# The two maps of differential attention combined by one VectorE instruction, and the output projection and norms of a hybrid encoder layer laid out anew

## The chip, the cores and the metric

The kernel runs on one core of a Trainium2 chip. The metric is the device time of one execution in microseconds (us). The kernel before took 3208.94 us (median of three runs, 3205.79 to 3213.26). The execution that was profiled took 3200.6 us; its span, from the first to the last instruction, is 3198.8 us.

## The reference

One encoder layer on two sequences that share their weights: a prompt of 512 tokens and a sample of 1024, each token 1024 wide, float32 throughout.

```python
h = rmsnorm(x, norm_pre_mix)
q, k, v, z, xbc, dt, gates = split(h @ w_in)
# attention: 8 heads, two maps each; scores get a bias by relative position
p = softmax(q @ k.T * scale + bias)          # per head and map
att = rmsnorm((p[0] - lam * p[1]) @ v, subln_w) * (1 - lam_init)
y = ssd(conv(xbc), dt) ... gated by z, normed # the state-space branch
m = (g0 * (att @ w_proj_attn) + g1 * (y @ w_proj_ssm)) @ w_out
x = x + rmsnorm(m, norm_post_mix)
h = rmsnorm(x, norm_pre_ffn)
f = (silu(h @ w_gate) * (h @ w_up)) @ w_down  # d_ff = 2816
x = x + rmsnorm(f, norm_post_ffn)
```

## The kernel before, in words

Every large product is done with three matrix multiplications on operands split into a high and a low part (`split`, lines 134 to 146: a ScalarE copy makes the high part, a VectorE or GpSimd subtraction the low part; `gemm`, lines 167 to 170, issues the three). The 1536 tokens are three chunks of 512: chunk 0 is the prompt, chunks 1 and 2 are the sample. Intermediate results go to DRAM tensors (`att_d`, `part_d`, `x2_d`, `h2_d`, `ff_d` and others). All loads and stores are issued by one queue, SyncE's (SP), in order.

The order of instructions on each engine is not the order of the text: the tile framework schedules with a model of times. Each instruction has a place in the text, and of those that are ready in the model the one with the earliest place goes first; a tile of a pool is given out when one of its buffers is free. Once planned, each engine runs its list in order.

Stages, by the time in the profiled span:

- **Up to about 1340 us**: first norm, projections, attention of the prompt woven into them, convolution and state-space scan.
- **Attention of the sample** (about 1345 to 1842 us). `heads` calls `attention` for 8 heads of 8 query tiles. For a query tile and each of the two maps: score matmuls into PSUM, a VectorE instruction that adds the bias and finds the maximum (L297), Exp on ScalarE (L300). Then the maps are combined: reciprocal and scale (L303, L304), and pm0 + scale * pm1, whose first half is one VectorE instruction (L307) and whose second half is two GpSimd instructions (L306, L309). Eight transposes follow, split again (L316, L317), and the product with v. `run` weaves a generator, `side_work`, between the steps of attention: after each of the 64 steps it advances it by `RATIO` = 0.5 steps. Side work has 32 steps of 24 matmuls: the attention projection of the prompt and the state-space projection of all three chunks (`gated`), stored in `part_d`.
- **Output projection and norms** (1842 to about 2175 us). `load_merged(0)` makes the operand of the prompt; `att_scale(1)` computes the scale of the sample's attention when its last head is done and stores it in `r_d`; `load_att(c)` loads a head of a chunk and its scales, multiplies (L357) and splits, head by head, through three buffers of the tag `araw`. `merge(c)` projects the scaled attention of a sample chunk (8 blocks of 24 matmuls) and adds `part_d`. `out_proj` multiplies by `w_out` (16 blocks of 24 matmuls) into four tiles that stay in SBUF, and `norms` does both norms on these tiles, transposes the result (L1083) and stores it in `h2_d`. The operands are pairs of 16 KB tiles out of a pool `big` of seven.
- **Gate and up products** (2101 to about 2806 us), by a seven-product scheme: `Operands` builds seven operands of 768 tokens from `h2_d` (two groups of tokens), `weights(jb)` builds seven weight operands of one of 22 blocks, `gate_up` does the seven products of 12 matmuls and combines them. Two blocks of the first group (`NPRE`) come ahead of `norms(2)` in the text and use Tanh for silu; the other blocks use buffers of a pool `fw` that is opened after the pool `mp` of the norms has closed.
- **Down product and last norm** (from 2806 us).

The text's order in the third stage is this, and the change rewrites it:

```python
m0 = load_merged(0); att_scale(1, ...); aT1 = att(1)
t0 = out_proj(m0);   m1 = merge(1, aT1); norms(0, t0)
aT2 = att(2); t1 = out_proj(m1); m2 = merge(2, aT2); norms(1, t1)
ops = Operands(0, wk, "araw", 3); ops.build_first(); ops.build(("b21",), ...)
t2 = out_proj(m2); ops.build(("t4",), ...); ops.build(("b22",), ...)
# two gate_up blocks, norms(2, t2); pool fw opens; the other blocks
```

Of the kernel before, what the change touches and what calls it, by code (L numbers as in the profile page):

```python
# [10 lines left out]
F32 = mybir.dt.float32  # L11
# [7 lines left out]
P = 128  # L19
D = 1024  # L20
# [12 lines left out]
VSH = 4  # L33
PU = (1, 1)
OT = ("gt", 2)
NG = 2
YE = ("act_pool",) * 4
RATIO = 0.5
# [4 lines left out]
NPRE = 2  # L43
CB = (1, 1)
RWB = 7
NW = 0
NKEEP = 1
# [31 lines left out]
def hybrid_trunk_kernel(ctx: ExitStack, tc: tile.TileContext, a: dict, y_prompt, y_sample):  # L79
# [35 lines left out]
    part_d = dram.tile([D, T], F32, name="part_d")  # L115
    x2_d = dram.tile([T, D], F32, name="x2_d")
# [150 lines left out]
    def attention(base, SL, h, got, pend, zq, msq, qk, pp, at, qr, s_ps, t_ps, o_ps):  # L267
# [7 lines left out]
        for qc in range(SL // 512):  # L275
            ops = o_ps.tile([P, 512], F32, tag="o", name="o")
            for q2 in range(2):
                aT = [at.tile([P, 2, 4, 256], F32R, tag=f"aT{b0}", name="aT", bufs=2 - b0 // 4)
                      for b0 in range(0, nkb, 4)]
                for u in range(2):  # L280
# [24 lines left out]
                    ca, cb = slice(0, SL * VSH // 8), slice(SL * VSH // 8, SL)  # L305
                    G.tensor_scalar(pm[1][:, cb], pm[1][:, cb], zs[:, 1:2], 0.0, op0=ALU.mult, op1=ALU.add)  # L306
                    V.scalar_tensor_tensor(pm[0][:, ca], pm[1][:, ca], zs[:, 1:2], pm[0][:, ca],  # L307
                                           op0=ALU.mult, op1=ALU.add)
                    last_add.append(G.tensor_add(pm[0][:, cb], pm[0][:, cb], pm[1][:, cb]))  # L309
# [494 lines left out]
    zq, msq = [ap.tile([P, 8, 8], F32, name=n) for n in ("zq", "msq")]  # L804
    with ExitStack() as ph2:
# [62 lines left out]

        side = side_work()
# [7 lines left out]
    with ExitStack() as ph3:  # L877
        big = ph3.enter_context(tc.tile_pool(name="big", bufs=7, reuse_waits="tile"))
        wk = ph3.enter_context(tc.tile_pool(name="wk", bufs=2, reuse_waits="tile"))
        wy = ph3.enter_context(tc.tile_pool(name="wy", bufs=1, reuse_waits="tile"))  # L880
        mm = ph3.enter_context(tc.tile_pool(name="mm", bufs=6, space=PSUM, reuse_waits="tile"))
# [5 lines left out]

        def big_pair():
            return [big.tile([P, KB, 512], F32R, tag="big", name="big") for _ in range(2)]

        def load_merged(c):
            hi, lo = big_pair()
            for k in range(0, KB, 2):
                both = mp.tile([P, 2, 512], F32, tag="mt", name="both", bufs=4)
                load(out=both, in_=part_d[k * P:(k + 2) * P, c * 512:(c + 1) * 512].rearrange("(a p) t -> p a t", p=P))
                S.activation(out=hi[:, k:k + 2], in_=both, func=AF.Copy, scale=0.5)
                V.scalar_tensor_tensor(lo[:, k:k + 2], both, 0.5, f(hi[:, k:k + 2]), op0=ALU.mult, op1=ALU.subtract)
            return hi, lo
# [141 lines left out]
        with ExitStack() as ph3a:  # L1040
# [69 lines left out]
            for jb in range(NPRE):  # L1110
                gate_up(0, jb, ops.all(), w[jb], mp, 1, False)
# [105 lines left out]
```

## Time and profile before

| what | value |
|---|---|
| median of three runs | 3208.94 us |
| the profiled execution | 3200.6 us |
| its span | 3198.8 us |
| mean granted TensorE clock | 0.979 |
| TensorE matmul busy | 3040.4 us, 95% |
| VectorE busy | 1814.7 us, 57% |
| ScalarE busy | 1256.6 us, 39% |
| GpSimd busy | 880.0 us, 28% |
| DMA | 430.39 MB, 43.1% of 16 engines' span on SP's queue |

How to read the rows: "L307 DVE ... x64 | 66.5, 1039 | 1.6" is a group of 64 instructions of line 307 on VectorE, 66.5 us busy, 1039 ns each on the mean, with 1.6 us of idle time ahead of them. PE is TensorE, PEld its weight loads, DVE VectorE, ACT ScalarE, POOL GpSimd, SPq SyncE's queue. Matmuls are pipelined and their ends are modelled, so a busy PE is not a PE at its peak.

### The profile page before, as it was taken

How to read it: one execution, taken by the hardware profiler on the slowest of the kernel's cores; microseconds unless marked ns; L12 is line 12 of the kernel's file. 1: busy time of each engine (PE TensorE's matmuls, PEld its weight loads, DVE VectorE, ACT ScalarE, POOL GpSimd, SP SyncE). 2: the span in 40 equal slices, each digit the busy share in tenths (PEclk: the TensorE clock that was granted, in tenths of full speed). 3: DMA queues.
4: the chain of work that ended last, by engine and by line, in shares of the span. 5: the costliest groups of instructions: out<-in, count | busy, mean ns of one | idle time of the engine just before them, and what ended most of it. 6: DMA issues, size and time to landing. Idle time of an engine off the chain costs nothing. (4 is left out here: it accounts for less than half of the span.)

```text
span 3198.8 us, 44610 instructions
## 1 busy us (share of the span) xinstructions
PE 3040.4 (95%) x16667; PEld 2671.8 (84%) x16667; DVE 1814.7 (57%) x2953; ACT 1256.6 (39%) x2301; POOL 880.0 (28%) x712
## 2 busy tenths in 40 slices
PE   7999999999999999899999998979999899989998
PEld 7988887888887778677788787868999899978787
DVE  5214443455328995387777855686667766632444
ACT  4103333333303433366666645543333333332343
POOL 0003332000233442277655500023333433210100
PEclk9999999999999999999999999988999999999999
DMA  4633333123554445755545147644333333363454
GB/s 148 195 99 113 111 101 109 57 78 106 155 166 143 145 141 154 209 156 169 163 140 187 34 141 238 228 130 136 103 98 109 92 103 98 109 201 97 123 163 132
DMA packets 443170, 430.39 MB, mean 135 GB/s; under 512 B 25233, under 2 KB 360306, under 8 KB 441842
## 3 DMA queue, kind: packets, MB, share of 16 engines
q1 hardware_dynamic: 442953, 427.55, 43.1%
q8 instruction: 131, 2.15, 0.3%
q14 instruction: 86, 0.70, 0.1%
HBM read 315.40 MB, written 120.44 MB: 136 GB/s over the span
## 5 line engine op out<-in xcount | busy, mean ns | idle before, releaser
L168 PE MATMUL acc<-hT,whi 128*128 128x512 f32 x1056 | 422.6, 400 | 3.3 <-ACT st L458 3.3
L169 PE MATMUL acc<-hT,whi 128*128 128x512 f32 x1056 | 417.6, 395 | 0.0
L170 PE MATMUL acc<-hT,wlo 128*128 128x512 f32 x672 | 263.8, 392 | 0.0
L300 ACT ACTIVATE pt<-pt,nm 128x1024 f32<-128x1024 f32 (+1 forms) x192 | 193.2, 1007 | 125.1 <-DVE nm L297 115.3
L168 PEld LDWEIGHTS acc<-hT,whi 128*128 128x128 f32 x1056 | 199.6, 189 | 48.8 <-issue 5.8
L297 DVE CUSTOM_DVE_ANT_0 pt<-s,tb 128x1024 f32<-128x1024 f32 (+1 forms) x192 | 196.9, 1041 | 68.3 <-PE s L295 50.1
L169 PEld LDWEIGHTS acc<-hT,whi 128*128 128x128 f32 x1056 | 199.6, 189 | 42.5 <-issue 3.6
L168 PE MATMUL acc<-whi,hT 128*128 128x256 f32 x768 | 224.9, 293 | 0.9 <-ACT hT L207 0.5
L170 PE MATMUL acc<-whi,hT 128*128 128x256 f32 x768 | 224.6, 293 | 0.4 <-DVE hT L208 0.3
L169 PE MATMUL acc<-wlo,hT 128*128 128x256 f32 x768 | 223.8, 292 | 0.0
L170 PE MATMUL d<-dhi,fl 128*128 128x512 f32 x528 | 207.8, 394 | 8.7 <-DVE fl L137 8.7
L168 PE MATMUL d<-dhi,fh 128*128 128x512 f32 x528 | 207.5, 393 | 7.8 <-ACT fh L136 7.8
L169 PE MATMUL d<-dlo,fh 128*128 128x512 f32 x528 | 207.2, 392 | 0.0
L137 DVE TENSOR_TENSOR fl<-raw,fh 128x896 fp32r<-128x896 f32 (+1 forms) x72 | 86.0, 1195 | 200.1 <-ACT fh L136 200.1
L136 ACT CAST whi<-wraw 128x1024 fp32r<-128x1024 f32 (+1 forms) x115 | 116.0, 1037 | 201.1 <-PE acc L169 84.1
L168 PE MATMUL mm<-op,wy 128*128 128x384 f32 x528 | 178.8, 339 | 9.4 <-ACT op L136 8.9
L170 PE MATMUL mm<-op,wy 128*128 128x384 f32 x528 | 178.7, 338 | 0.0
L169 PE MATMUL mm<-op,wy 128*128 128x384 f32 x528 | 178.3, 338 | 0.0
L306 POOL TENSOR_SCALAR pt<-pt,zs 128x512 f32<-128x512 f32 (+1 forms) x96 | 94.3, 982 | 281.8 <-DVE zs L304 240.3
L137 DVE TENSOR_TENSOR wlo<-wraw,whi 128x1024 fp32r<-128x1024 f32 x80 | 95.4, 1222 | 114.2 <-ACT whi L136 104.9
L136 ACT CAST fh<-raw 128x896 fp32r<-128x896 f32 (+1 forms) x72 | 70.7, 982 | 227.3 <-PE d L169 212.7
L170 PE MATMUL acc<-hT,whi 128*128 128x512 f32 x384 | 157.3, 410 | 0.0
(360 smaller groups left out, 8452.8 us busy)
## 6 DMA issues: line engine op xcount, KB each, us to landing
wraw<-in_w_in_dram SPq DMA_DIRECT2D x60, 512.0 KB
wraw<-in_w_gate_up_dram SPq DMA_DIRECT2D x92, 256.0 KB
raw<-ff_d SPq DMA_DIRECT2D x48, 448.0 KB
wr<-in_w_gate_up_dram SPq DMA_DIRECT2D x80, 256.0 KB
ff_d<-c SPq DMA_DIRECT2D x88, 192.0 KB
g_d<-st SPq DMA_DIRECT2D x48, 256.0 KB
xg<-xs_d SPq DMA_DIRECT2D x48, 256.0 KB
gt<-g_d SPq DMA_DIRECT2D x48, 256.0 KB
```

The source lines that it names most:

```text
L136: S.copy(hi, raw)
L137: V.tensor_sub(lo, raw, f(hi))
L168: TE.matmul(ps, ah, bh, start=(i == 0), stop=False)
L169: TE.matmul(ps, ah, bl, start=False, stop=False)
L170: TE.matmul(ps, al, bh, start=False, stop=(i == n - 1))
L297: V.tensor_tensor_reduce(out=pt[:], in0=sps[:], in1=tb[:, off:off + SL], scale=-1.0, scalar=3.0e38, op0=ALU.add, op1=ALU.min, accum_out=nm ...
L300: S.activation(out=pt, in_=pt, func=AF.Exp, bias=nm[:, m:m + 1], scale=-1.0, accum_out=(z0, zs[:, 0:1])[m])
L306: G.tensor_scalar(pm[1][:, cb], pm[1][:, cb], zs[:, 1:2], 0.0, op0=ALU.mult, op1=ALU.add)
```

## The change

- **Maps.** The combination of the two maps is one VectorE instruction on the whole width; GpSimd does none of it. `VSH` goes.
- **Side work.** The prompt's output projection becomes 16 more steps of the side work, through the one PSUM buffer `f`; `RATIO` is 0.75. Its operand `m0` takes the side work's tile `yT`.
- **Norms through memory.** `out_proj` stores its result in a new DRAM tensor `mo_d`; `norms` is a generator of 16 steps that loads 128x512 pieces of it (tag `nt`, four buffers, which `merge` uses for `pt` too), stores `x2_d` by halves, loads it again for the second norm, transposes and stores `h2_d`. The norms of the last chunk are advanced by one step after each gate-and-up block.
- **Operands.** The pool `big` has nine pieces of 12 KB. An operand of gate and up is one piece; a pair for a projection is three (`Part` finds the place). Each operand loads its own terms (40 loads a group rather than 20), all additions are VectorE's, and raw tiles come from `fw` (six buffers).
- **Pools.** `mp` is gone, `fw` is open for the whole stage; no block is done ahead with Tanh.

```diff
-RATIO = 0.5
+RATIO = 0.75
...
-                    ca, cb = slice(0, SL * VSH // 8), slice(SL * VSH // 8, SL)
-                    G.tensor_scalar(pm[1][:, cb], pm[1][:, cb], zs[:, 1:2], 0.0, op0=ALU.mult, op1=ALU.add)
-                    V.scalar_tensor_tensor(pm[0][:, ca], pm[1][:, ca], zs[:, 1:2], pm[0][:, ca],
-                                           op0=ALU.mult, op1=ALU.add)
-                    last_add.append(G.tensor_add(pm[0][:, cb], pm[0][:, cb], pm[1][:, cb]))
+                    last_add.append(V.scalar_tensor_tensor(pm[0], pm[1], zs[:, 1:2], pm[0], op0=ALU.mult, op1=ALU.add))
...
+    def out_proj(c, mT, pool, psum):
+        for p0 in range(0, D, 256):
+            w = split_panel(a["w_out"][0][:, p0:p0 + 256])
+            for j in range(4):
+                ps = psum()
+                gemm_tm(ps, w, mT, slice(j * P, (j + 1) * P))
+                mo = pool.tile([P, 512], F32, tag="gt", name="mo")
+                S.copy(mo[:, 0:256], ps)
+                S.activation(out=mo[:, 256:512], in_=ps, func=AF.Square, accum_out=sums[c][:, j, p0 // 256:p0 // 256 + 1])
+                r0 = c * 512 + j * P
+                store(out=mo_d[r0:r0 + P, p0:p0 + 256], in_=mo[:, 0:256])
+                yield
...
+            m0 = yt.tile([P, 2, KB, 512], F32R, tag="yT", name="m0", bufs=1)
+            for k in range(0, KB, 2):
+                both = rp.tile([P, 2, 512], F32, tag="wraw", name="both")
+                load(out=both, in_=part_d[k * P:(k + 2) * P, 0:512].rearrange("(a p) t -> p a t", p=P))
+                S.activation(out=m0[:, 0, k:k + 2], in_=both, func=AF.Copy, scale=0.5)
+                V.scalar_tensor_tensor(m0[:, 1, k:k + 2], both, 0.5, f(m0[:, 0, k:k + 2]), op0=ALU.mult, op1=ALU.subtract)
+            yield from out_proj(0, (m0[:, 0], m0[:, 1]), yt, lambda: f_ps.tile([P, 512], F32, tag="f", name="f")[:, 0:256])
...
-        big = ph3.enter_context(tc.tile_pool(name="big", bufs=7, reuse_waits="tile"))
+        big = ph3.enter_context(tc.tile_pool(name="big", bufs=9, reuse_waits="tile"))
...
-            return [big.tile([P, KB, 512], F32R, tag="big", name="big") for _ in range(2)]
+            tiles = [big.tile([P, 2, 3, 512], F32R, tag="big", name="big") for _ in range(3)]
+            return Part(tiles, 0), Part(tiles, 1)
...
-                    pt = wk.tile([P, 512], F32, tag="pt", name="pt", bufs=1)
+                    pt = wk.tile([P, 512], F32, tag="nt", name="pt", bufs=4)
...
+        def norms(c):
...
+            for j, t, o in places:
+                mo, xt = nt_tile("mo"), nt_tile("xt")
+                load(out=mo, in_=mo_d[t * P:(t + 1) * P, o:o + 512])
+                load(out=xt, in_=rows(t, a["x_prompt"], a["x_sample"])[:, o:o + 512])
+                V.scalar_tensor_tensor(mo, mo, r[:, 0, j:j + 1], pmw[:, o:o + 512], op0=ALU.mult, op1=ALU.mult)
+                V.tensor_add(mo, mo, xt)
+                S.activation(out=xt, in_=mo, func=AF.Square, accum_out=s2[:, j, o // 512:o // 512 + 1])
+                store(out=x2_d[t * P:(t + 1) * P, o:o + 512], in_=mo)
+                yield
...
+            for j, t, o in places:
+                xn = nt_tile("xn")
+                load(out=xn, in_=x2_d[t * P:(t + 1) * P, o:o + 512])
+                V.tensor_scalar(xn, xn, r[:, 1, j:j + 1], 0.0, op0=ALU.mult, op1=ALU.add)
+                ps = tr_ps.tile([P, 4, P], F32, tag="tr", name="tr_ps")
+                for i in range(4):
+                    TE.transpose(ps[:, i, :], xn[:, i * P:(i + 1) * P], ident)
+                hr = nt_tile("hr")
+                for i in range(4):
+                    k = C_FFN + o // P + i
+                    S.activation(out=hr[:, i * P:(i + 1) * P], in_=ps[:, i], func=AF.Copy, scale=cols[:, k:k + 1])
+                store(out=h2_d[o:o + 512, t * P:(t + 1) * P].rearrange("(k p) t -> p k t", p=P),
+                      in_=hr[:].rearrange("p (k t) -> p k t", t=P))
+                yield
...
+        att_scale(1, zq, msq, ap, tr_ps, "tr")
+        aT1 = att(1)
+        run(norms(0))
+        m1 = merge(1, aT1)
+        aT2 = att(2)
+        run(out_proj(1, m1, wk, lambda: mm_tile(256)))
+        m2 = merge(2, aT2)
+        run(norms(1))
+        ops = Operands(0, fw, "rw", RWB)
+        ops.build(ops.names[:5])
+        run(out_proj(2, m2, wk, lambda: mm_tile(256)))
+        ops.build(ops.names[5:])
+        last = norms(2)
+        w = {}
+        for jb in range(FB):
+            w[jb] = weights(jb)
+            gate_up(0, jb, ops.all(), w[jb])
+            next(last, None)
+        ops = Operands(768, fw, "rw", RWB)
+        ops.build(ops.names)
+        for jb in reversed(range(FB)):
+            if jb < FB - 1:
+                w[jb] = weights(jb)
+            gate_up(768, jb, ops.all(), w[jb])
```

More of the change, by code (lines that the diff above doesn't have):

```diff
@@ L804, in hybrid_trunk_kernel @@
     zq, msq = [ap.tile([P, 8, 8], F32, name=n) for n in ("zq", "msq")]
+    sums = [ap.tile([P, 4, 4], F32, name=f"sums{c}") for c in range(NCH)]
+    def out_proj(c, mT, pool, psum):
[10 more added lines that the diff above has]
+                yield
     with ExitStack() as ph2:
@@ L886, in mm_tile, with __init__, __getitem__ @@
             return mm.tile([P, n], F32, tag="mm", name="mm")
-        def big_pair():
-            return [big.tile([P, KB, 512], F32R, tag="big", name="big") for _ in range(2)]
[L891 to L898, printed above, removed]
+        class Part:
+            def __init__(self, tiles, part):
+                self.tiles, self.part = tiles, part
+            def __getitem__(self, at_):
+                return self.tiles[at_[1] // 3][(at_[0], self.part, at_[1] % 3) + at_[2:]]
+        def big_pair():
+            tiles = [big.tile([P, 2, 3, 512], F32R, tag="big", name="big") for _ in range(3)]
+            return Part(tiles, 0), Part(tiles, 1)
         def merge(c, aTt):
@@ L972, in weights @@
             for k0 in (0, 4):
-                if rpool is not None and k0 == 0:
-                    raw = rpool.tile([P, 4, 256], F32, tag="wr", name="wr", bufs=1)
+                if k0 == 0:
+                    raw = fw.tile([P, 4, 256], F32, tag="wr", name="wr", bufs=1)
                 else:
@@ L1114, in hybrid_trunk_kernel @@
-        with tc.tile_pool(name="fw", bufs=2, reuse_waits="tile") as fw:
-            for jb in range(NPRE, FB):
-                if jb >= NPRE + NW:
-                    w[jb] = weights(jb, rpool=fw if jb > NPRE else None)
-                gate_up(0, jb, ops.all(), w[jb], fw, 2)
-            ops = Operands(768, fw, "rw", RWB)
-            ops.build_first()
-            ops.build(ops.names[4:], G, "act_dve")
-            for jb in reversed(range(FB)):
-                if jb < FB - NKEEP:
-                    w[jb] = weights(jb, rpool=fw)
-                gate_up(768, jb, ops.all(), w[jb], fw, 2)
+        pmw = fw.tile([P, D], F32, name="pmw", bufs=1)
@@ new lines, in att @@
+        def att(c):
+            return load_att(c, big_pair(), lambda: [
+                wk.tile([P, 512], F32, tag="araw", name="araw", bufs=3) for _ in range(2)])
+        att_scale(1, zq, msq, ap, tr_ps, "tr")
[9 more added lines that the diff above has]
+        run(out_proj(2, m2, wk, lambda: mm_tile(256)))
```

143 lines of the change are left out of this document (31 added, 112 removed).

## The prediction

> **What bounds the kernel now.** I read the page first, then the busy time in stretches, because a mean over stages with different limits says little.
>
> ```profile
> span 3198.8 us, 44610 instructions
> PE 3040.4 (95%) x16667; PEld 2671.8 (84%) x16667; DVE 1814.7 (57%) x2953; ACT 1256.6 (39%) x2301; POOL 880.0 (28%) x712
> ```
>
> TensorE is the bound: 158.4 us of the span are left for a change that removes no matmul. The second view shows in which stretches of the changed part they lie (busy us and instructions of PE, PEld, DVE, ACT, POOL; then the granted clock, DMA share, GB/s).
>
> ```profile
> core 0: us, PE busy (x) PEld busy (x) DVE busy (x) ACT busy (x) POOL busy (x), PEclk, DMA share, GB/s
> 1345.00:1741.00 396.00, 373.68 (x2065) 315.84 (x2066) 303.83 (x495) 255.78 (x403) 252.12 (x178) 0.99 0.53 158
> 1741.00:1842.00 101.00, 88.31 (x542) 74.40 (x540) 85.01 (x158) 66.10 (x115) 55.40 (x46) 0.95 0.26 85
> 1842.00:1896.00 54.00, 49.68 (x396) 49.48 (x395) 23.54 (x41) 23.42 (x56) 0.00 (x0) 0.94 0.41 132
> 1896.00:1945.00 49.00, 46.15 (x194) 37.02 (x194) 38.96 (x64) 24.86 (x51) 0.00 (x0) 0.97 0.78 270
> 1945.00:2007.00 62.00, 53.77 (x417) 52.01 (x416) 24.09 (x42) 30.14 (x73) 0.00 (x0) 0.94 0.56 181
> 2007.00:2101.00 94.00, 93.19 (x609) 85.38 (x608) 64.64 (x115) 53.29 (x121) 0.00 (x0) 1.00 0.64 209
> 2101.00:2210.00 109.00, 79.35 (x407) 74.18 (x406) 85.28 (x143) 44.31 (x88) 43.89 (x28) 0.83 0.46 144
> 2210.00:2450.00 240.00, 240.00 (x1375) 240.00 (x1374) 148.42 (x263) 83.89 (x163) 83.98 (x67) 1.00 0.34 101
> 2450.00:2500.00 50.00, 38.95 (x202) 37.28 (x201) 45.66 (x70) 22.85 (x48) 26.15 (x18) 0.90 0.33 99
> ```
>
> I count as lost in a stretch its idle PE time, plus the busy time times what the clock lacks. Attention with side work, 1345 to 1741: 22.3 + 0.01 x 373.7 = 26 us. Its end, where no side work is left, to 1842: 12.7 + 0.05 x 88.3 = 17. First output projection: 4.3 of plain idle time. Second, 1945 to 2007: 8.2 + 0.06 x 53.8 = 11.5. Start of gate and up, 2101 to 2210: 29.7 + 0.17 x 79.4 = 43. Change of token groups, 2450 to 2500: 11.0 + 0.10 x 39.0 = 15. Together 117 us, and the change touches all of it. Between the last two, 240 us show no idle time at all.
>
> **The maps.** Groups of the stretch 1345 to 1845, and one of the whole page:
>
> ```profile
> L307 DVE SCALAR_TENSOR_TENSOR pt<-pt,zs 128x512 f32<-128x512 f32 x64 | 66.5, 1039 | 1.6
> L137 DVE TENSOR_TENSOR whi<-wraw,whi 128x1024 fp32r<-128x1024 f32 x28 | 43.5, 1552 | 10.8 <-ACT whi L136 10.8
> ...
> L309 POOL TENSOR_TENSOR pt<-pt 128x512 f32<-128x512 f32 x64 | 84.4, 1319 | 4.6
> L306 POOL TENSOR_SCALAR pt<-pt,zs 128x512 f32<-128x512 f32 x64 | 72.5, 1133 | 151.6 <-DVE zs L304 127.5 <-ACT aT L316 12.8 <-ACT km L240 4.6
> ...
> L137 DVE TENSOR_TENSOR wlo<-wraw,whi 128x1024 fp32r<-128x1024 f32 x80 | 95.4, 1222 | 114.2 <-ACT whi L136 104.9
> ```
>
> Removed: 64 x (1.133 + 1.319) = 157 us of POOL, and 2.45 us of latency per query tile. The new instruction, 128x1024 with two inputs from SBUF, is nowhere in the trace. Nearest is line 137 on 128x1024: 1.222 us where POOL rests, 1.552 where it works beside it. I take 1.222, since half of POOL's work in this stretch goes: DVE pays 64 x (1.222 - 1.039) = +12 us (at 1.552: +33), and gets back 28 x 0.33 = 9 when line 137 too falls to its price beside an idle POOL. DVE's 388.8 us of the 497 in the first two stretches stay about the same, so the edit costs nothing on DVE; what hides it is TensorE, 93% busy there. Without that cover it would cost those 12 to 33 us. Its worth is that a tile is ready for its transposes 2.45 - 1.22 = 1.2 us sooner; this counts only in the fill below. In the prompt's attention TensorE has no gap at all:
>
> ```profile
> 200.00:500.00 300.00, 300.00 (x1457) 251.06 (x1456) 116.08 (x263) 86.91 (x177) 91.85 (x96) 1.00 0.34 110
> ```
>
> So I put 0 there, between -3 and +3.
>
> **Side work: the first output projection goes under attention.** In 1842 to 1896 its 384 matmuls make up nearly all of 396, and of 49.7 us of PE; I count 48. Moved, they push the last attention matmul back by 48 less what they fill. There is 26 + 17 = 43 us to fill, so the bounds are 0 and 43. The last step of today's side work ends here, 100 us before attention does:
>
> ```profile
> 1740.09 0.68 DVE L830 SCALAR_TENSOR_TENSOR gt<-gt,f 128x512 f32<-128x512 f32 x1
> ```
>
> I take 25: nearly all of the 17 behind that row, and a third of the 26, since the chain of a tile gets shorter while one PSUM buffer still serializes the side steps. Net +23. The evacuations (two ACT instructions a step) and the 16 stores move along; in the queue they stand among attention's q and k loads. The operand m0 brings four DVE instructions, 1.2 us each by line 137's row.
>
> **What it uncovers.** Today the 47.8 us hide the loading of the sample's attention. The timeline around it:
>
> ```profile
> 1842.21 0.59 ACT L324 COPY av<-o 128x512 f32<-128x512 f32 x1 [4.80 <-PE o L170]
> ...
> 1863.14 0.75 DVE L357 SCALAR_TENSOR_TENSOR araw<-araw,cols 128x512 f32<-128x512 f32 x1 [6.06 <-DMA araw<-r_d]
> ...
> 1884.99 0.75 DVE L357 SCALAR_TENSOR_TENSOR araw<-araw,cols 128x512 f32<-128x512 f32 x1 [0.25 <-DMA araw<-r_d]
> ...
> 1890.91 0.75 DVE L357 SCALAR_TENSOR_TENSOR araw<-araw,cols 128x512 f32<-128x512 f32 x1 [3.79 <-DMA araw<-r_d]
> ...
> 1894.84 0.75 DVE L357 SCALAR_TENSOR_TENSOR araw<-araw,cols 128x512 f32<-128x512 f32 x1 [1.79 <-DMA araw<-r_d]
> ```
>
> From the last attention output (1842.2) to the first head's multiplication is 21 us, then eight heads follow at 31.7 / 7 = 4.5 us each, a round trip of two loads through three buffers; with the last multiplication and split, about 2 us, it is 55. About 3 fall away, since m0's four instructions (4.9 us) no longer run among the scale's: 52. `merge(1)` needs all eight heads for every block, and PE's whole list stands behind it. Its eight blocks are the 46 busy us of 1896 to 1945, but while heads drip in, the four blocks whose two weight panels fit their buffers can run along. So after the last head remain 23 us plus about 5 for the next panel's split, or 46 if the planned order takes block after block; I take 32, nearer the first, since the planner takes what is ready. From the last attention matmul to the end of `merge(1)`: 84 us, against 1945 - 1842.2 = 102.8 now. That is -19, with bounds 80 (-23) and 98 (-5); heads at 6.5 us instead of 4.5, should the new loads of `norms(0)` stand between theirs, add 16. With the +23 above, this half of the change gives **+4 us**.
>
> A rule for this gap stands in the Trainium skill, page "TensorE: Matmul & The Clock Gate", section "What's actually happening": after about 3.4 us without work the clock falls to half, and comes back after as much dense work. The granted 0.83 beside 29.7 us of idle time fits it. By an estimate from that page the bare wait costs 1.7 us more when the last head comes, and the sum would rise by that; no row isolates it.
>
> **Norms through memory.** The second output projection loses 11.5 us today to transposes of `norms(0)` that stand in PE's queue. Changed, they fall into the wait before `merge(1)`: -8, between 0 and -15. `norms(1)` gets later: its pieces share four buffers with `merge(2)`'s `pt`, which stands earlier in the text, and its data go to DRAM and back twice.
>
> **Start of gate and up.** What PE waits for there today:
>
> ```profile
> 2117.50 0.69 PE L168 MATMUL mm<-op,whi 128*128 128x384 f32 x1 [14.15 <-ACT whi L136]
> ...
> 2163.77 2.59 PE L1083 MATMUL tr_ps<-ident,mt 128*128 128x128 f32 x8 [6.84 <-DVE mt L1079]
> ...
> 2174.92 0.45 PE L168 MATMUL mm<-op,whi 128*128 128x384 f32 x1 [2.39 <-ACT whi L136]
> ```
>
> The first is a weight operand that came late, the next the transposes of `norms(2)`, the last the weights after them. With raw tiles in `fw`, no POOL split of b22, and the norms spread over blocks, all three causes go. What is late next is the operands that need `norms(1)`. Six pieces are free once `merge(2)` ends; a row of the stretch 2210 to 2450 prices an addition or a split on 128x384:
>
> ```profile
> L1014 DVE TENSOR_TENSOR c<-c,c 128x384 f32<-128x384 f32 x33 | 18.4, 559 | 1.7
> ```
>
> t2 takes 12 of these, t3 and t1 8 each, t4 16: 44 x 0.56 = 25 us of DVE after the first half of `norms(1)`, which I place near the end of `out_proj(2)`; products need the first of them 2 us later. I leave 14 of the 43 us standing: -29 (bounds -38 and 0).
>
> **Norms among the blocks.** The loop of the weights is nearly as long as PE's. The chain of waits, one turn of it:
>
> ```profile
> 2289.89 1.30 POOL s L995
> 2291.63 4.15 DMA wr<-in_w_gate_up_dram
> ...
> 2304.32 1.30 POOL s L995
> ```
>
> A turn is 14.43 us; a block's 84 matmuls at 1375 in 240 us are 14.66. So 0.23 us a block is all the room that ACT, DVE and SP's queue have for a step of `norms(2)` (two loads and a store, or one and one, the store waiting for DVE, with the next weight loads behind it). A step that delays the loop by 0.75 us costs 0.5 x 16 = **+8**; bounds 0 and +32 (2.2 us a step).
>
> **Change of groups.** With nine pieces two operands of the second group can be built ahead; the other five follow the release of one piece per product (2.1 us). t4 on DVE is last: -8 of the 15, bounds -13 and 0.
>
> **Sum.** +4 - 8 - 29 + 8 - 8 = -33 us on 3200.6 us of the profiled execution: 3167.6. The median of the runs stands 8.3 us above that execution, so 3176. What a measurement of this kernel can tell from no change is about 0.2%, 6.4 us: 3202.5 to 3215.4.
>
> **Rivals.**
> - *Side work covers the wait.* If steps of the output projection are still left when attention ends, they run under the 52 us. Some 34 us of the wait vanish: 3142. For it: the side work was planned to the end of the text and PE takes the earliest ready. Against: today it was used up 100 us early.
> - *The bare wait decides, slower.* Place: from the last attention matmul to `merge(1)`. If the fill is 0 (+25), the blocks are taken one by one (+14) and heads come at 6.5 us behind `norms(0)`'s loads (+16), it is 3231. It passes the old time when these make 33 us. For it: the head at 1890.91 came 5.9 us after the one before it. Against: the 17 us at the end of attention are plainly for lack of side work.
> - *The weights' loop.* At 2.2 us a step 32 us instead of 8: 3200. For it: 0.23 us of room. Against: the steps use no POOL, and DVE is 62% and ACT 35% busy there.
> - *Operands no earlier.* If `norms(1)` is so late that gate and up lose 43 us as now, this part doesn't do what it says: 3205. For it: four shared buffers. Against: TensorE needs the first late operand only after `merge(2)` and `out_proj(2)`, 94 us.
>
> **How the numbers follow.** Forecast 0.45 (its own range 3150 to 3200), covered wait 0.15, bare wait 0.20, weights' loop 0.10, operands 0.10. The range 3120 to 3228 takes in the covered wait with some microseconds more and all but the worst of the bare one. Faster by over 0.2%: nearly all of the forecast, the covered wait, and half of the last two, 0.68. Within: 0.13. Slower: nearly all of the bare wait, 0.19.
>
> **What would show it.** Maps: one group of 64 at 1.2 to 1.3 us on DVE in attention, POOL near 150 us there. Side work: the last attention output near 1865, matmuls of the output projection up to it. Wait: PE idle some 50 us before the merge's blocks, released by the splits of `araw` heads. Gate and up: first idle time there by operands, not by weights. Loop: blocks of the first group over 14.7 us while `norms(2)` runs. Wrong if PE shows no such wait, or if weights end idle time between blocks.

## The result, and the profile after

The changed kernel takes 3250.91 us (median of four runs, 3248.44 to 3258.09), the kernel before 3207.66 in the runs beside it: a ratio of 1.0133, with a 95% interval of 1.0117 to 1.0148. The forecast was 3176, between 3120 and 3228; the time lies above the range.

First the page of the changed kernel, its span, its busy times and its DMA, whose line for the kernel before said 430.39 MB:

```profile
span 3250.0 us, 44579 instructions
PE 3057.7 (94%) x16667; PEld 2678.2 (82%) x16667; DVE 1861.0 (57%) x2985; ACT 1266.9 (39%) x2373; POOL 662.8 (20%) x504
DMA packets 473697, 457.14 MB, mean 141 GB/s; under 512 B 27600, under 2 KB 386225, under 8 KB 472369
```

As many matmuls, 217 us less of GpSimd, 46 us more of VectorE, 26.75 MB more traffic. The span is 51.2 us longer. The starts and ends of TensorE's stages in the two traces show where (us from the span's start; the last column runs on):

| mark on TensorE | before | after | after is behind by |
|---|---|---|---|
| sample's attention, ninth matmul of its first product with v | 1380.2 | 1374.2 | -6.0 |
| end of its last matmul | 1842.2 | 1876.7 | 34.5 |
| end of `merge(1)` | 1944.9 | 1963.1 | 18.2 |
| end of `out_proj(1)` | 2007.0 | 2028.8 | 21.8 |
| first gate and up product | 2101.1 | 2135.1 | 34.0 |
| start of the fourth block | 2189.2 | 2232.5 | 43.3 |
| start of the second group | 2468.1 | 2525.7 | 57.6 |
| end of the last gate and up product | 2806.2 | 2855.5 | 49.3 |

The busy time in stretches, cut at these marks (columns as in the prediction), answers to the view shown there:

```profile
core 0: us, PE busy (x) PEld busy (x) DVE busy (x) ACT busy (x) POOL busy (x), PEclk, DMA share, GB/s
1345.00:1849.00 504.00, 481.87 (x2826) 417.86 (x2825) 397.67 (x628) 325.85 (x548) 152.66 (x93) 0.98 0.49 148
1849.00:1877.00 28.00, 23.98 (x161) 21.07 (x159) 21.63 (x45) 14.90 (x28) 0.00 (x0) 0.94 0.32 92
1877.00:1902.00 25.00, 1.45 (x9) 1.10 (x9) 13.24 (x36) 6.92 (x17) 0.00 (x0) 0.59 0.83 258
1902.00:1963.10 61.10, 53.82 (x220) 40.47 (x220) 28.05 (x49) 19.87 (x46) 0.00 (x0) 0.94 0.72 223
1963.10:2028.80 65.70, 49.73 (x389) 48.99 (x390) 33.85 (x45) 31.01 (x73) 0.00 (x0) 0.87 0.63 199
2028.80:2073.60 44.80, 44.80 (x194) 35.90 (x194) 24.71 (x42) 17.85 (x31) 0.00 (x0) 1.00 0.58 185
2073.60:2135.10 61.50, 50.47 (x393) 49.86 (x393) 30.11 (x51) 30.61 (x87) 3.10 (x3) 0.92 0.67 213
2135.10:2201.20 66.10, 37.87 (x110) 24.76 (x109) 51.65 (x93) 29.15 (x72) 15.71 (x10) 0.56 0.80 252
2201.20:2232.60 31.40, 29.70 (x170) 29.38 (x170) 26.42 (x54) 13.01 (x28) 9.17 (x7) 1.00 0.45 143
```

Two things stand out. The woven part of attention is 108 us longer than before (504 against 396) and has just as much idle time, 22.1 us against 22.3; the end without side work shrank from 101 us to 28, and its idle time from 12.7 us to 4.0. And the first gate and up block takes 66 us with 38 of work, at a granted clock of 0.56 and with the DMA engines 80% busy. What TensorE waits for, in the timeline of the third stage:

```profile
1880.10 1.05 PE L322 MATMUL ms<-onec,av 128*128 128x1 f32 x8 [3.42 <-ACT av L319]
1891.14 0.39 PE L337 MATMUL rt<-ident,att_r 128*64 128x128 f32 x1 [9.99 <-DVE att_r L335]
1902.03 2.08 PE L163 MATMUL mm<-big,whi 128*128 128x512 f32 x4 [10.49 <-ACT big L131]
...
1977.69 0.58 PE L163 MATMUL mm<-whi,big 128*128 128x256 f32 x1 [11.80 <-DVE gt L931]
...
2086.94 0.58 PE L163 MATMUL mm<-whi,big 128*128 128x256 f32 x1 [4.46 <-ACT big L933]
...
2121.89 1.11 PE L1067 MATMUL tr_ps<-ident,xn 128*128 128x128 f32 x4 [6.53 <-DVE xn L1064]
...
2145.54 1.09 PE L1067 MATMUL tr_ps<-ident,xn 128*128 128x128 f32 x4 [4.80 <-DVE xn L1064]
2149.58 1.08 PE L1067 MATMUL tr_ps<-ident,xn 128*128 128x128 f32 x4 [2.96 <-DVE xn L1064]
2161.25 0.69 PE L163 MATMUL mm<-op,whi 128*128 128x384 f32 x1 [2.76 <-ACT op L131]
2180.58 0.69 PE L163 MATMUL mm<-op,wlo 128*128 128x384 f32 x1 [2.32 <-ACT op L131]
2190.36 0.69 PE L164 MATMUL mm<-op,wy 128*128 128x384 f32 x1 [2.04 <-DVE op L132]
```

The first three are the bare wait that was foretold. The fourth stands between `merge(1)` and `out_proj(1)`: the results of the merge are evacuated late (taken out of PSUM, line 931, and added to `pt`, line 932). `pt` shares its four buffers with the pieces of `norms(0)`, which hold them. So the first two evacuations of `merge(1)`, at 1937.6 us, wait for a `pt` that is loaded from 1960.0 on; they hold both buffers of `gt` meanwhile, and the later blocks' loads of `gt` come only after them:

```profile
1937.62 1.28 DVE L931 SCALAR_TENSOR_TENSOR gt<-gt,mm 128x512 f32<-128x512 f32 x2
...
1967.30 1.34 DVE L932 TENSOR_TENSOR gt<-gt,pt 128x512 f32<-128x512 f32 x2
```

```profile
1960.00 6.24 SPq L928 DMA_DIRECT2D pt<-part_d  x3
```

At the start of gate and up the waits are for the transposes of `norms(1)` and then for one operand after the other. Those transposes (line L1083 before, L1067 after) in the groups of their tiles, first the kernel before, then the one after:

```profile
L1083 PE MATMUL tr_ps<-ident,mt x32: 271/272/328, 2052.1 to 2070.8; 128*128 128x128 f32 x32
```

```profile
L1053 DVE SCALAR_TENSOR_TENSOR mo<-mo,mr,pmw x8: 751/752/753, 2067.3 to 2109.7; 128x512 f32<-128x512 f32 x8
...
L1067 PE MATMUL tr_ps<-ident,xn x32: 270/421/477, 2121.9 to 2165.9; 128*128 128x128 f32 x32
```

19 us before, all inside `out_proj(2)`'s stretch; 44 us after, ending 31 us into gate and up.

### The profile page after: what moved, and what is told of

It is laid out like the page before. It is cut to its first block, busy times and chain, and to the rows that moved or that the text cites. A ratio compares the mean times of both kernels' runs of the same rounds, so it can differ in the third digit from the quotient of the medians.

```text
span 3250.0 us, 44579 instructions
## 1 busy us (share of the span) xinstructions
PE 3057.7 (94%) x16667; PEld 2678.2 (82%) x16667; DVE 1861.0 (57%) x2985; ACT 1266.9 (39%) x2373; POOL 662.8 (20%) x504
## 4 chain that ended last, share of the span: by engine, by line
PE 66%; DMA 14%; DVE 9%; ACT 4%; issue 4%; POOL 2%; SPq 1%; ACTq 0%; DVEq 0%; POOLq 0%
PE acc L163 9%; PE acc L165 9%; PE acc L164 9%; PE mm L163 5%; PE mm L164 5%; PE mm L165 5%; PE d L165 4%; PE d L163 3%; PE d L164 3%; DMA gt<-g_d 2%; DMA araw<-r_d 1%; PE t L304 1%; DMA wraw<-in_w_gate_up_dram 1%; PE s L289 1%; DMA raw<-k_d 1%
## 5 line engine op out<-in xcount | busy, mean ns | idle before, releaser
L131 ACT CAST whi<-wraw 128x1024 fp32r<-128x1024 f32 x112 | 114.2, 1049 | 217.1 <-PE acc L164 82.5
L997 POOL TENSOR_TENSOR s<-wr,wraw 128x512 f32<-128x512 f32 x43 | 56.3, 1308 | 649.8 <-DMA wraw<-in_w_gate_up_dram 293.2
L230 POOL TENSOR_TENSOR ql<-raw,qh 128x512 fp32r<-128x512 f32 x48 | 66.5, 1400 | 584.0 <-ACT qh L227 514.1
```

Of the source, the lines that this page charges most:

```text
L131: S.copy(hi, raw)
L230: G.tensor_sub(q_l[:, s_], q_r[:, s_], f(q_h[:, s_]))
L997: G.tensor_add(s1, a21, a22)
```

## The experiments

All ratios are to runs of the kernel before on the same chip; 0.1% is 3.2 us, and a point is a percent of the kernel before. The kernel called `pieces` is before with the two parts of the change that helped, and stands as the base of several others.

| kernel | median us | ratio, 95% interval |
|---|---|---|
| the changed kernel | 3250.91 | 1.0133, 1.0117 to 1.0148 |
| maps_alone | 3193.21 | 0.9971, 0.9952 to 0.9990 |
| pieces | 3181.35 | 0.9953, 0.9939 to 0.9966 |
| pieces_npre3 | 3182.15 | 0.9934, 0.9908 to 0.9960 |
| side_alone | 3206.20 | 1.0015, 0.9996 to 1.0035 |
| norms_mem | 3231.74 | 1.0088, 1.0057 to 1.0120 |
| norms_mem8 | 3214.39 | 1.0038, 1.0022 to 1.0054 |
| norms_mem_q | 3243.22 | 1.0131, 1.0113 to 1.0149 |
| one_trip | 3206.30 | 1.0011, 0.9999 to 1.0024 |
| share | 3233.66 | 1.0092, 1.0064 to 1.0119 |
| op0_cover | 3255.52 | 1.0158, 1.0126 to 1.0189 |
| op0_phases | 3236.01 | 1.0114, 1.0095 to 1.0133 |
| phases | 3260.61 | 1.0198, 1.0177 to 1.0218 |
| n1_early | 3255.62 | 1.0158, 1.0127 to 1.0190 |
| q_pool | 3257.38 | 1.0161, 1.0136 to 1.0186 |
| nt6 | 3277.41 | 1.0247, 1.0228 to 1.0266 |

**One part alone: the maps.**

```diff
-  three instructions (L306, L307, L309)
+  last_add.append(V.scalar_tensor_tensor(pm[0], pm[1], zs[:, 1:2], pm[0], op0=ALU.mult, op1=ALU.add))
```

> The kernel before with the maps combined by one VectorE instruction, and nothing else of the change. Theory (the maps are worth next to nothing): the instruction takes 1.43 us, as in the changed kernel's trace, and not 1.22; VectorE has room for it, a tile is ready some 1 us sooner, and the time is 3200 to 3210 us. Rival (the longer instruction is what slows the changed kernel): 64 x (1.43 - 1.04) = 25 us more VectorE work on the path of the sample's attention and as much in the prompt's, 3220 to 3235 us.

Measured: faster by 0.29%, 0.10 to 0.48%. The time, 3193.21 us, lies 7 us below the first expectation, but the kernel before took only 3200.89 us on that chip. The instruction costs 1.43 us, as both said, and the time is not longer for it. Its group, and that of the weights' low parts beside it:

```profile
L305 DVE SCALAR_TENSOR_TENSOR pt<-pt,zs 128x1024 f32<-128x1024 f32 x64 | 91.5, 1429 | 1.3
...
L137 DVE TENSOR_TENSOR whi<-wraw,whi 128x1024 fp32r<-128x1024 f32 x28 | 36.6, 1307 | 17.3 <-ACT whi L136 17.2
```

In this trace the sample's attention takes 458.6 us from the mark in its first product to its last matmul, 462.0 before: 3.4 of some 9 us. The rest lies between the two attentions; there the trace of `pieces`, whose text is the same up to that point, is 9 us later (1381.6 against 1372.3), so this rest isn't put down to the maps.

**One part alone: nine pieces for operands**, and on top of it a third early block.

```diff
-  big = pool(name="big", bufs=7)          # pieces of 16 KB
+  big = pool(name="big", bufs=9)          # [P, 2, 3, 512], three for a pair
...
-  ops.build_first()
-  ops.build(ops.names[4:], G, "act_dve")
+  ops.build(ops.names, V, "act_dve")      # second group
```

> The kernel before with the maps in one instruction and the nine pieces of 12 KB for operands, without the side work and without the norms through memory. Theory (these two are the parts of the change that help): the maps give 8 us as measured alone, and the change of groups goes from 28 to 21 us as in the changed kernel, so 3183 to 3188 us, less than before by some 0.5%. Rival (the pieces help only where nothing else does): 3190 to 3196 us, as with the maps alone.

> The kernel 'pieces' (3181 us) with three gate and up blocks ahead of norms(2) in the text instead of two. Theory (the third block takes 34 us instead of 15 because the transposes of norms(2) stand in TensorE's list before their data): another block ahead of them hides most of it, 3166 to 3176 us. Rival (the weight operands, whose buffers are few before fw is open, are as late for a third early block): 3178 to 3190 us.

Measured for `pieces`: 0.47% faster than before; its interval overlaps that of the maps alone, so the step from one to the other rests on the trace. The block at the change of groups takes 15.7 us instead of 29.6 (28.0 in maps_alone), more than was expected; in the changed kernel it takes 20.6. A third early block (NPRE = 3) adds nothing that the intervals separate (the rival): the three blocks of 36, 17 and 34 us become four of 36, 24, 15 and 29. `pieces` is faster than the kernel before and the changed one.

**One part alone: the prompt's output projection as side work.**

```diff
-RATIO = 0.5
+RATIO = 0.75
...
+  yield from side_proj(0, m0, ...)        # 16 steps, results to mo_d
...
-  t0 = out_proj(m0)
+  for j in range(4): load(out=t0[j], in_=mo_d[j * P:(j + 1) * P, :])
```

> The kernel 'pieces' (3181 us) with the prompt's output projection as side work at ratio 0.75; its result goes to mo_d and is loaded back once, as four whole tiles, for norms(0); the norms themselves stay in SBUF. Theory of the prediction (a net +4 up to merge(1), and -8 in out_proj(1) because the transposes of norms(0) fall into the wait): 3175 to 3180 us. Rival (the fill of attention is only some 10 us, as the changed kernel shows, so that merge(1) ends 18 us later): 3190 to 3202 us.

Measured: 0.62 points slower than `pieces` (1.0015 against 0.9953), 20 us: the rival, whose range the time passes by 4 us. In the trace attention grows from 459.9 to 495.6 us, so the 48 us of added matmuls fill 12 us. From the last attention matmul to the end of `merge(1)` it is 83.6 us, 100.2 in `pieces`. `out_proj(1)` takes 59.6 us instead of 64.1 in `pieces`: its loss from the transposes of `norms(0)` got smaller.

**Undoing that part in the changed kernel.**

```diff
-RATIO = 0.75
+RATIO = 0.5
...
+  m0 = big_pair()                         # loaded as in load_merged
   att_scale(1, ...); aT1 = att(1)
+  run(out_proj(0, m0, wk, lambda: mm_tile(256)))
   run(norms(0))
```

> The changed kernel with the prompt's output projection taken out of the side work (ratio 0.5 again) and put after attention, where it stood before; all the rest stays as changed. Theory (the bare wait before the merge costs 18 us, which is what the changed kernel is behind at the end of merge(1)): merge(1) ends near 1945 us instead of 1963, and of this all or most stays: 3233 to 3241 us, the upper end if the transposes of norms(0) fall back among the second output projection. Rival (the whole loss stands behind merge(1), in norms(1)): merge(1) ends earlier but gate and up starts as late as before, 3247 to 3253 us.

Measured: 1.0158, nearest the rival, whose range the time passes by 2 us, and no gain at all. The theory was right up to `merge(1)`, which ends at 1938.1 instead of 1963.1. Then 46 us pass before `out_proj(1)`. TensorE's waits in the timeline of this kernel, from 1938 to 1984:

```profile
1940.51 0.66 PE L1060 MATMUL tr_ps<-ident,xn 128*128 128x128 f32 x4 [2.40 <-DVE xn L1057]
1944.69 1.12 PE L1060 MATMUL tr_ps<-ident,xn 128*128 128x128 f32 x4 [3.52 <-DVE xn L1057]
1949.82 1.08 PE L1060 MATMUL tr_ps<-ident,xn 128*128 128x128 f32 x4 [4.01 <-DVE xn L1057]
1956.46 1.08 PE L1060 MATMUL tr_ps<-ident,xn 128*128 128x128 f32 x4 [4.16 <-DVE xn L1057]
1967.68 1.08 PE L1060 MATMUL tr_ps<-ident,xn 128*128 128x128 f32 x4 [8.30 <-DVE xn L1057]
1984.08 0.58 PE L163 MATMUL mm<-whi,big 128*128 128x256 f32 x1 [12.91 <-DVE gt L924]
```

The transposes of `norms(0)` stand in TensorE's list between the two products, and each comes at the pace of a load from `x2_d`. In the changed kernel the wait for the sample's attention hides most of them; with that wait covered they are bare. The last row is another wait, that of the changed kernel: `merge(1)` is not evacuated, since the pieces of `norms(0)` hold the buffers of `pt`, whose loads come from 1970.5 us on:

```profile
1970.50 4.44 SPq L921 DMA_DIRECT2D pt<-part_d  x3
```

So the transposes are not all that `out_proj(1)` waits for.

**Other places in the text for the norms.**

```diff
-  m2 = merge(2, aT2)
-  run(norms(1))
+  run(norms(1))                           # n1_early
+  m2 = merge(2, aT2)
```

```diff
-  run(norms(0))                           # phases; op0_phases: on op0_cover
+  n0 = norms(0); run(islice(n0, 8))
   m1 = merge(1, aT1); aT2 = att(2)
   run(out_proj(1, ...))
+  run(n0); n1 = norms(1); run(islice(n1, 8))
   m2 = merge(2, aT2)
-  run(norms(1))
+  run(n1)
```

> The changed kernel with norms(1) written ahead of merge(2). Theory (norms(1) starts late because its four pieces go first to the pt of merge(2), which stands earlier in the text): its first load of mo moves from 2063 us to near 2035, the operands of gate and up come 25 to 30 us sooner, and most of the 53 us that the first block now loses vanish: 3220 to 3230 us. Rival (the one DMA queue and the round trips set its pace, wherever it stands): 3245 to 3255 us. Second rival (merge(2) now starves for its pt instead): over 3255 us.

> op0_cover again (prompt's output projection after attention), and the two phases of the norms parted in the text: the first phase of norms(0), which has no transposes, stays where it is, the second goes behind out_proj(1); the first phase of norms(1) goes ahead of merge(2), the second stays behind it. Theory (TensorE works its list in order, and the transposes of norms(0) stand in it before their data have made two trips through DRAM): in op0_cover TensorE waited 36 us in eight gaps beside these transposes, between merge(1) (end 1938 us) and out_proj(1) (start 1984); parted, out_proj(1) starts near 1945, and 25 to 40 us go: 3215 to 3230 us. Rival (not the place in TensorE's list but the traffic and the buffers of the norms hold everything up): the gap comes back elsewhere, 3245 us or more.

> The changed kernel with the phases of the norms parted in the text in the same way, and nothing else. Theory (transposes in TensorE's list): the sample's heads no longer share VectorE and the queue with the second phase of norms(0), merge(1) ends up to 5 us sooner and out_proj(1) loses less, but the second phase of norms(0) now stands among merge(2) and competes there with norms(1): 3230 to 3245 us. Rival (the wait that covers norms(0) in the changed kernel is the only cheap place for it): 3250 to 3270 us.

`n1_early` is no faster than the changed kernel: 3255.62 us lies at the border of its two rivals, and the trace shows the second one, a `merge(2)` that starves for its `pt`. The mechanism of the theory works and the gain is lost again. `norms(1)` starts at 2033.1 us and is through at 2101.2, in 68 us instead of 99, and the first block of gate and up takes 24 us instead of 66; but 38 us appear ahead of `out_proj(2)`, which starts at 2111.7 instead of 2073.4. That stretch of this kernel, and the wait that ends it:

```profile
2073.70:2111.70 38.00, 7.21 (x29) 4.72 (x28) 10.21 (x17) 12.15 (x34) 0.00 (x0) 0.54 0.61 193
```

```profile
2111.71 0.58 PE L163 MATMUL mm<-whi,big 128*128 128x256 f32 x1 [10.07 <-DVE gt L931]
```

The first two evacuations of `merge(2)` run at 2032.1 and 2035.6 us; the loads of `pt` that their additions need are issued only when `norms(1)` gives its buffers back, and the additions follow:

```profile
2098.88 3.10 SPq L928 DMA_DIRECT2D pt<-part_d  x3
```

```profile
2101.73 0.69 DVE L932 TENSOR_TENSOR gt<-gt,pt 128x512 f32<-128x512 f32 x1 [1.33 <-DMA pt<-part_d]
```

`phases` is slower still (its rival), by a hole of 45 us at the same place, where the first `pt` is loaded at 2088.5 us. `op0_phases` gains 0.44 points on `op0_cover` (the intervals overlap at 1.0126 to 1.0133), less than its theory wanted: `out_proj(1)` starts at 1949.8, and 26.6 us come back ahead of `out_proj(2)`:

```profile
2085.47 0.58 PE L163 MATMUL mm<-whi,big 128*128 128x256 f32 x1 [26.60 <-DVE gt L924]
```

In all four orders, as in the changed kernel, a merge waits for `pt` while the norms' pieces hold the four buffers; moving the norms moves that wait. (In side_alone, where `pt` keeps its own buffer, an addition follows its evacuation by 1.2 us, from 1929.5 to 1930.7.) Buffers of its own for `pt`, and nothing else, were not tried in the changed kernel. They can't be the whole answer: the next kernel has them, shows no such hole and loses 43 us all the same.

**One part alone: norms through memory, on `pieces`.**

```diff
-  t1 = out_proj(m1); ...; norms(1, t1)    # tiles in SBUF
+  run(out_proj(1, m1, ...)); ...; run(norms(1))   # the changed kernel's out_proj and norms, nt: 4 buffers
```

> The kernel 'pieces' (before, with one-instruction maps and nine pieces; 3181 us) with the changed kernel's norms through memory put in: out_proj stores to mo_d, norms loads, stores x2_d, loads it again, four buffers nt of their own, while pt keeps its own buffer; text order, no side work, operands and Tanh blocks as in before. Theory (norms through memory are what costs: norms(1) takes 106 us in the changed kernel from its first multiplication to its last store, 59 in the kernel before): 3215 to 3245 us. Rival (the loss comes from the rest: one pool, pt sharing nt, 40 raw loads for the operands): 3180 to 3195 us.

Measured: 1.0088 against 0.9953, 1.35 points or 43 us: the theory. `norms(1)` starts at once here (2017.9, since `pt` keeps its own buffer), and still takes 96 us to its last transpose (2114.1), 56 in `pieces` (2012.7 to 2068.7). The stretches of `out_proj(2)` and of the start of gate and up, first `pieces` (two stretches of it), then `norms_mem`:

```profile
2049.10:2099.10 50.00, 49.74 (x418) 49.43 (x417) 29.99 (x48) 32.36 (x83) 0.00 (x0) 1.00 0.55 178
2099.10:2151.50 52.40, 32.76 (x171) 30.83 (x169) 46.75 (x73) 20.97 (x48) 23.86 (x14) 0.84 0.45 143
```

```profile
2046.00:2104.80 58.80, 52.60 (x410) 51.16 (x409) 29.82 (x56) 31.51 (x93) 0.00 (x0) 0.94 0.74 224
2104.80:2177.80 73.00, 36.43 (x178) 33.56 (x177) 60.05 (x113) 31.02 (x73) 22.74 (x15) 0.70 0.59 183
```

The first two blocks take 21 us more, `out_proj(2)` 9 more, and the four blocks behind them 10. Three kernels ask what it is in the norms that costs:

```diff
-  mp.tile([P, 512], F32, tag="nt", name=name, bufs=4)
+  mp.tile([P, 512], F32, tag="nt", name=name, bufs=8)    # norms_mem8; and bufs=2 for 4 in load_merged
```

```diff
-  load(out=mo, in_=mo_d[...]); ... store(...)            # the five DMAs of norms
+  G.dma_start(out=mo, in_=mo_d[...]); ...                # norms_mem_q
```

```diff
-  S.copy(tiles[j][:, p0:p0 + 256], ps)                   # one_trip: pieces, but
+  store(out=mo_d[...], in_=mo[:, 0:256])                 # out_proj stores
+  load(out=tiles[j], in_=mo_d[r0:r0 + P, :])             # norms loads whole tiles, then as before
```

> The kernel 'norms_mem' (norms through memory in the layout of before, 3232 us against 3181 without) with eight buffers nt instead of four, and two instead of four for the raw tiles of load_merged. Theory 1 (four buffers of pieces set the pace: with two pieces under way, each buffer is held for a load, an instruction and a store): norms(1) takes 75 us instead of 100, 3200 to 3215 us. Theory 2 (the traffic: 6.3 MB more for each chunk, in a stretch whose DMA engines are 69% busy) and theory 3 (order in the one queue): 3226 to 3238 us.

> The kernel 'norms_mem' with the five DMAs of the norms issued by GpSimd, which is idle there, instead of SyncE. Theory 3 (the one queue, in which a store that waits for an engine stands ahead of the next loads): 3200 to 3215 us. Theories 1 and 2 (buffers, traffic): 3226 to 3240 us.

> The kernel 'pieces' (3181 us) with the first trip of the norms alone: every out_proj stores its result to mo_d, and norms loads it back as four whole tiles of 128x1024; after that the norms work on these tiles in SBUF as before. Theory 2 (traffic; this has 4.2 of the 6.3 MB a chunk): two thirds of the 50 us, 3207 to 3220 us. Theory 1 (small pieces through few buffers; here there are none): 3185 to 3198 us, by the latency of one store and one load.

Eight buffers bring back 0.50 points, 16 us. They shorten the first phase alone. Its additions are L1084; first `norms_mem`, then `norms_mem8`:

```profile
L1084 DVE TENSOR_TENSOR mo<-mo,xt x8: 679/682/693, 2020.3 to 2058.6; 128x512 f32<-128x512 f32 x8
```

```profile
L1084 DVE TENSOR_TENSOR mo<-mo,xt x8: 685/691/693, 2021.1 to 2041.3; 128x512 f32<-128x512 f32 x8
...
L1097 PE MATMUL tr_ps<-ident,xn x32: 271/272/329, 2053.3 to 2105.9; 128*128 128x128 f32 x32
```

38 us become 20, but the transposes still need 53 (48 with four buffers). So the time is in the range of theory 1, while `norms(1)` takes 88 us rather than the 75 that it named. Another queue does not help: on GpSimd's the kernel is 0.43 points slower; whether order in one queue costs anything is not settled by that, since GpSimd's own price is in it. One trip in whole tiles costs 0.58 points, 19 us, below the range of the traffic theory and above that of the buffers. Of the 43 us, then, some 16 go with eight buffers, and some 19 come with one trip and no small pieces at all; how much of these 19 is traffic and how much the time of a trip was not separated. Why the second phase keeps its pace with eight buffers stays open; in every one of these traces its transposes stand among the blocks of `out_proj(2)`.

The same two questions had been put to the changed kernel itself, less cleanly:

```diff
-  tag="nt", bufs=4 (pt and norms); RWB = 6
+  tag="nt", bufs=6;                RWB = 3   # nt6
```

> The changed kernel with the five DMAs of the norms (loads of mo, x and x2, stores of x2 and h2) issued by GpSimd instead of SyncE; order and buffers stay. Theory (SyncE's queue, in which stores that wait for ScalarE or VectorE stand ahead of the norms' loads, sets the pace): the first phase and second phase of norms(1) each take 20 us less, norms(2) no longer holds up the weights (14 us), 3215 to 3230 us. Rival (buffers and round trips set it): 3245 to 3255 us.

> The changed kernel with six buffers for the pieces of the norms and of merge's pt instead of four, paid for with three raw buffers for operands instead of six. Theory (four buffers set the pace of the norms, 6 us a piece in the second phase of norms(1), which holds two buffers a piece): a piece takes 4 us, norms(1) is through 25 to 30 us sooner and the first block of gate and up loses as much less: 3220 to 3232 us. Rival (round trips through DRAM and the one queue set it): 3245 to 3256 us. Three raw buffers may cost some microseconds at the change of groups, which is read apart.

`q_pool` (the diff of norms_mem_q, on the changed kernel) gained nothing. `nt6` is 1.14 points slower than the changed kernel, 37 us, which neither theory named: `norms(1)` is through 10 us sooner, but with three raw buffers the operands' chain lasts from 2133 to 2227 us, the first block takes 84 us and the change of groups 37. The operands have a chain of their own, then.

**The raw loads of the operands.**

```diff
-  ops.build(ops.names[:5])
+  ops.build_first()                       # b11, t2, t3, t1 from shared raw tiles
+  ops.build(ops.names[4:5])
```

> The changed kernel with the first four operands of the first group built together from shared raw tiles as before (20 loads from h2_d instead of 40, 32 fewer VectorE additions at most). Theory (the chain of raw loads and additions for the operands, 2145 to 2200 us, holds up the first gate and up block): the block takes 45 to 52 us instead of 66, 3230 to 3240 us. Rival (the last store of norms(1), near 2170 us, holds it up): the block stays at 60 us or more, 3245 to 3255 us.

Measured: 1.0092 against 1.0133, 0.41 points or 13 us (the intervals overlap at 1.0117 to 1.0119); the first block takes 49.9 us instead of 66.1, as the theory had it. The stretch of that block in this kernel:

```profile
2130.00:2180.00 50.00, 29.10 (x111) 22.65 (x110) 41.57 (x81) 26.84 (x68) 16.78 (x10) 0.73 0.70 212
```

## Why the prediction was wrong, step by step

**The sum of the parts**, in points against before: maps -0.29, pieces -0.18, side work +0.62, norms through memory +1.35, twice the raw loads in the first group +0.41. That is +1.91; the whole change is +1.33. The 0.58 between them, 19 us, is probably overlap: `norms(0)` lies under the wait that the side work uncovered, and op0_cover, which covers the wait, pays for it. No run isolates this, and the parts without a run of their own (`pt` in the norms' buffers, no early blocks with Tanh, the last norms among the blocks) are in the difference too.

**The sum of the stages**, from the table of marks: +18.2 us up to `merge(1)` (forecast +4), +3.6 in `out_proj(1)` (-8), +12.2 in `merge(2)` and `out_proj(2)` (nothing), +9.3 in the first three blocks (-29), +14.3 in the rest of the first group (+8), -8.3 in the second (-8). That is +49.3 where -33 was forecast. The largest misses are the start of gate and up, 38 us, and the side work, 14.

- **Maps, 0 (±3).** Right in kind, and small. 1.43 us lies inside the bounds of 1.222 to 1.552, above the value taken. The kernel gained some 9 us by the ratio, 3.4 of them in the sample's attention.
- **Fill of 25 us.** The first step that failed. It was 12 alone; in the changed kernel attention takes 43.9 us more than in maps_alone, so 4. The end without side work was filled about as foretold (8.7 of its 12.7 us of idle time). The third of the 26 us in the woven part was not: its idle time stays at 22 us, over 108 us more, and its granted clock went from 0.99 to 0.98. Why the added steps left it there is open.
- **The wait, 84 us from the last attention matmul to the end of `merge(1)`.** Right: 86.4, with two small misses that cancel: the first head's multiplication comes 23.8 us after the last attention matmul (18 by the prediction's terms), the heads follow at 4.6 us each, and `merge(1)` ends 30.5 us after the last of them starts (about 34). The net of this half was to be +4 and is +18, nearly all from the fill.
- **`out_proj(1)`, -8.** It is +3.6. The transposes did leave it (59.6 us in side_alone, 64.1 in `pieces`), but in the changed kernel TensorE stands still for 11.8 us because `merge(1)` is not evacuated. The prediction saw that `pt` and the norms share four buffers and let the norms wait for `pt`; in `merge(1)` it is `pt` that waits for the norms. The lower bound of this term, -15, was also more than the 11.5 us that the stretch lost.
- **`norms(1)` "gets later", left without a price.** The step that decided. The prediction said that the data go to memory and back twice and that four buffers are shared, and then placed the first half of the norms near the end of `out_proj(2)` without a row. Their length was the term: from the first multiplication to the last transpose 57 us before (2014.1 to 2070.8), 99 after (2067.3 to 2165.9), and 96 in norms_mem, where the trip and its buffers are what is new; there it costs 43 us. The first half is stored some 7 us after `out_proj(2)` ends at 2135 us (its last store is issued at 2142.0), the second 33 us after (2168.5). An earlier start was tried only together with a starved `merge(2)` (n1_early), so what the late start costs by itself isn't known.
- **`merge(2)` and `out_proj(2)`, no term.** They take 106.3 us instead of 94.1. Two waits make up 11.0 of the 12.2: 4.5 us for the last evacuation of `merge(2)`, and 6.5 us for the first transposes of `norms(1)`.
- **Start of gate and up, -29.** It is +9.3 (53.3 us lost against 44.0). The causes named for before did go; no weight operand ends a long wait there now. What came late next was named too, but sized by VectorE's 25 us alone. The chain of raw loads, additions and splits lasts from 2145 to 2200 us, 55 us where 25 were priced, through six buffers and 40 loads a group, and starts when the first half of `norms(1)` is stored. The first eight steps of `norms(2)` run beside it (2170.9 to 2207.5). Against "TensorE needs the first late operand only after 94 us" stands that `norms(1)` needs 137 from the end of `out_proj(1)`.
- **Norms among the blocks, +8.** It is +14.3, by another cause, so the size is luck. Some 4 of that are no delay: eight blocks with four transposes each take 15.1 to 15.2 us instead of 14.7, and these matmuls only moved here. Three blocks of 15.8 to 18.8 us make up most of the rest. They come after the last transposes (2427.2), while VectorE builds the operands of the second group and waits 7.9 us for their raw tiles; no step of `norms(2)` and no weights hold them up.
- **Change of groups, -8.** The block is 9 us shorter, and 12 to 14 in `pieces`; in the changed kernel the three blocks just named pay about as much for the same operands.

The rival "operands no earlier" described the case, four shared buffers included, and was given 0.10 and a price of 3205, because it let gate and up lose 43 us "as now" rather than more. The rivals were priced one at a time, and the range had room for one: 3205 for this, 3231 for the worst of the bare wait. Here a poor fill and late operands came together.

## What to carry to other kernels

A tile that leaves SBUF and comes back has to be priced by its whole chain (load, instruction, store, release of the buffer, times the pieces over those under way) and by what stands behind it in the in-order list of the engine that consumes it. Two chains that share a tag of buffers wait for each other, in either direction: in the four orders tried here, moving one in the text moved the wait. Work that is to fill idle time may leave it where it is, as the 22 us in the woven part, and work that is taken from one stage uncovers what it hid. Parts of a joint change are worth trying singly: here two of the five that were tried so helped, and `pieces` with these two is 0.47% faster than before.

## What was not expected of the hardware

**VectorE beside GpSimd.** The mean of 1.43 us for the new instruction hides two prices. In the sample's attention of the changed kernel, 49 of the 64 such instructions meet no GpSimd work and take 1.28 us on the mean; 11 that overlap it in part take 1.73, and four that are overlapped through 90% or more take 2.39. One of each kind on VectorE, and the GpSimd instructions around the slow one:

```profile
1373.29 1.28 DVE L300 SCALAR_TENSOR_TENSOR pt<-pt,zs 128x1024 f32<-128x1024 f32 x1
...
1413.61 2.40 DVE L300 SCALAR_TENSOR_TENSOR pt<-pt,zs 128x1024 f32<-128x1024 f32 x1
```

```profile
1410.16 3.40 POOL L138 TENSOR_TENSOR yTt<-yraw,yTt 128x1024 fp32r<-128x1024 f32 x1
1413.64 3.53 POOL L238 TENSOR_TENSOR km<-raw,km 64x512 fp32r<-64x512 f32 x2
```

The instructions of line 292, which read PSUM and are as wide, take 1.22 us with and without GpSimd beside them. The Trainium skill, page "GPSIMD Engine Reference", section "Specifications", says that GpSimd's interfaces to SBUF are shared with VectorE and contended by VectorE instructions with two SBUF inputs. The trace agrees, and adds that the slowed one takes nearly twice its time.

**The queue of a transfer.** The kernel was slower with the norms' DMAs on GpSimd's queue (1.0131 against 1.0088), though GpSimd is idle in norms_mem from 2000 to 2104.8 us (0.00 us busy). The norms did not get longer: `norms(1)` takes 94 us there from its first multiplication to its last transpose, 96 in norms_mem, but it starts 29 us after the end of `out_proj(1)` rather than 18. Why is open. The Trainium skill, page "DMA: Bandwidth & Descriptors", section "Issuing engine by pattern", gives simple loads and stores to SyncE; the times of the two kernels agree.
